# Attention in two matmul forms: products of 64 columns per query block, or split products of 256 and 384 columns per key block, with more weights split ahead of the joins

## The chip, the cores and the metric

One core of a Trainium2 chip runs the whole kernel. The metric is device microseconds of that core for one execution, as the median of several runs. The engines are named as in the profile: PE multiplies matrices, DVE, ACT and POOL work on vectors, SP starts transfers.

## The reference

Two layers of an encoder on an input of 512 rows x 1024, all in fp32. Each layer adds three blocks to x, each with a norm before it and one behind:

```
x = x + 0.5 * rms_norm(swiglu(rms_norm(x, nw[0]), ...), nw[1])
m = even_mixer(...) if l % 2 == 0 else odd_mixer(...)
x = x + rms_norm(m, nw[3])
x = x + 0.5 * rms_norm(swiglu(rms_norm(x, nw[4]), ...), nw[5])
```

swiglu has 2816 inner columns. The even mixer joins a pooling of 256 columns with attention: 12 query heads of 64 columns, 4 heads of keys and values, and each block of 128 queries sees the blocks before, at and behind it, with a sink term in the denominator:

```
m = jnp.maximum(jnp.max(s, axis=-1, keepdims=True), sk)
p = jnp.exp(s - m)
denom = jnp.sum(p, axis=-1, keepdims=True) + jnp.exp(sk - m)
o = jnp.einsum('bnhgqk,bnkhd->bnqhgd', (p / denom).astype(v.dtype), vw)
```

The odd mixer joins a gated convolution with a state-space scan in two directions, whose output y becomes rms_norm(y * silu(z)).

## The kernel before, in words

The stages run in the order f00 (FFN), even mixer, f01, f10, odd mixer, f11. x lives in SBUF as four row blocks of 128. An fp32 matrix product is done as three products of rounded halves (mm3: high x high, high x low, low x high), each through mm. split makes the halves of an activation: ACT casts the high half (xh), DVE subtracts it for the low half (xl). Weights come through one queue of blocks, class Stream: a DMA brings a raw block, pump has ACT cast it (whi, L118) and DVE subtract (wlo, L119). The function keep marks blocks that an earlier FFN splits instead; pump writes those halves to DRAM and reads them back at their turn. Before, such blocks are those of the two mixers alone (KEEP 6 and 24).

Nothing is issued as the code stands: each part is a generator that yields either a time to wait (in ns of PE cost, counted as matmuls are issued: CHAIN, PWAIT, AVWAIT, UWAIT), or an event, or Need(n), n free ones of the eight PSUM banks. A planner runs the generators against that count, and so writes the order of instructions of every engine. Each engine then runs its own order, and waits on semaphores of the others.

Attention, in even(): heads goes over six pairs of query heads c and four query blocks n. unit(c, n) issues the scores of both heads (ev_s), the maxima (mx, L679), the bias (nm, L680), the exponentials with their sums (ev_p, L684), the sink terms (ex, L689), sum and reciprocal (rs, L691 and L692), the transposes of the probabilities by 128x128 blocks (ev_pT), their copies to SBUF (ev_pTs, L702 on ACT, L704 on DVE), the products with the values in plain fp32 (ev_av, 64 columns each, the probabilities as the stationary side), and the scaling by the reciprocal (ev_o, L715). Up to DEPTH = 3 units are under way at once. pair_end transposes the four outputs of a pair (ev_oT) and splits them into two row blocks of the mixer's output (ev_mh, ev_ml). Projections (ev_q, ev_u) and the output projection (evo_y) run between the units.

At the end of a stage down calls finish for each row block: squares (L462), the weighted copy (L463), the norm's factor (rstd, L428 on DVE, L430 on POOL), the addition to x (L471). norm_t follows with the next stage's norm (L438, L440), waits CHAIN[kind], and issues the transposes (evon_tp after the even mixer) and their split (L402). f_g and f_u are the FFN's matmuls behind them. wrow loads the norm's weight rows, and halves those of an FFN on POOL.

In odd(), the z projection (od_z) is made of four blocks of 256 columns for four row blocks, each evicted in 256 columns (L1190, L1174).

Of the kernel before, what the change touches and what calls it, by code (L numbers as in the profile page):

```python
# [7 lines left out]
F32 = mybir.dt.float32  # L8
# [22 lines left out]
DEPTH = 3  # L31
CHAIN = (12500, 8000, 13000)
# [10 lines left out]
ESPLIT = (3, 3)  # L43
# [7 lines left out]
ZBATCH = (4, 8)  # L51
# [3 lines left out]
KEEP = (6, 24)  # L55
DWB, LNG, LNB, CVB, CVW = 0, 4, 8, 12, 28
# [167 lines left out]
def odd_blocks(d):  # L224
# [16 lines left out]
    for b in range(4):  # L241
        out.append(dict(key=("z", b), src=w[:, :, 1024 + 256 * b:1280 + 256 * b], shape=(KC, 256),
                        parts=[(slice(0, 4), full(256)), (slice(4, 8), full(256))]))
# [22 lines left out]
class Gen:  # L266
# [151 lines left out]
    def wrow(self, src, name, half):  # L418
# [6 lines left out]
    def rstd(self, ss, n, name):  # L425
# [29 lines left out]
    def finish(self, t, src, banks, wpost, wnext, scratch, name, eng, kind):  # L455
# [11 lines left out]
        r = self.rstd(s1, D, f"{name}_p{t}")  # L467
# [142 lines left out]
    def even(self):  # L610
# [3 lines left out]
        with ExitStack() as es:  # L614
# [23 lines left out]
            v = [T(f"v{t}", [P, 256]) for t in range(NT)]  # L638
# [13 lines left out]
            def unit(c, n, av):  # L652
# [9 lines left out]
                ps, pss = [], []  # L662
                scs = []
# [18 lines left out]
                for e in range(2):  # L682
                    p = T("p", [P, 384], name=f"p{c}_{n}{e}", bufs=2 * DEPTH)
# [9 lines left out]
                self.free(*scs)  # L693
                yield PWAIT[c > 0]
                yield Need(2)
                for e in range(2):
                    pT = self.psum(f"ev_pT{c}_{n}{e}")
                    for b in range(nk // P):
                        self.tp(pT, pT[:, b * P:(b + 1) * P], ps[e][:, b * P:(b + 1) * P])
                    pTs = T("pTs", [P, 384], name=f"pTs{c}_{n}{e}", bufs=4)  # L700
                    if e == 0:
                        nc.scalar.copy(out=pTs[:, :nk], in_=pT[:, :nk])  # L702
                    else:
                        nc.vector.tensor_copy(out=pTs[:, :nk], in_=pT[:, :nk])  # L704
                    self.free(pT)
                    pss.append(pTs)
# [6 lines left out]
                o = T("o", [P, P], name=f"o{c}_{n}", bufs=2 * NT)  # L713
                for e in range(2):
                    nc.vector.tensor_scalar(out=o[:, 64 * e:64 * e + 64], in0=av[:, n * P + 64 * e:n * P + 64 * e + 64],  # L715
                                            scalar1=rs[:, e:e + 1], scalar2=0.0, op0=ALU.mult, op1=ALU.add)
                self.os[c, n] = o

            def heads():

                us = []
                for c in range(6):
                    yield qready[c]
                    yield Need(1)
                    av = self.psum(f"ev_av{c}")
# [7 lines left out]
            def pair_end(c, av, us):  # L733
                for u in us:
                    yield u
                self.free(av)
                yield 600
                yield Need(1)
                oT = self.psum(f"ev_oT{c}")
                for n in range(NT):  # L740
                    self.tp(oT, oT[:, n * P:(n + 1) * P], self.os.pop((c, n)))
                self.split(mix[2 + c][0], mix[2 + c][1], oT)
                self.free(oT)
                yield 1200
                mready[2 + c].done = True
# [8 lines left out]
            def pool(c, p):  # L754
                u = T("u", [P, 16 + S + 16], name=f"u{c}", bufs=2)
                a = T("sa", [P, 16 + S + 16], name=f"sa{c}", bufs=2)
# [37 lines left out]
            self.os, fa = {}, {}  # L794
# [10 lines left out]
            for t in range(NT):  # L805
# [3 lines left out]
                nc.scalar.copy(out=v[t], in_=pv[:, 0:256])  # L809
# [56 lines left out]
    def odd(self):  # L866
# [6 lines left out]
        with ExitStack() as es:  # L873
# [293 lines left out]
            zw = {}  # L1167

            def zblock(b, t):
# [3 lines left out]
                sz = self.scr.tile([P, 256], F32, tag="sg", name=f"od_sz{b}{t}")  # L1173
# [226 lines left out]
```

## Time and profile before

| what | us |
|---|---|
| median of 3 runs (lowest, highest) | 2007.65 (2005.86, 2009.3) |
| the profiled execution | 2007.16 |
| its span, from the first to the last instruction | 2005.4 |
| PE busy | 1980.2 |
| DVE busy | 971.3 |
| ACT busy | 761.8 |
| POOL busy | 64.5 |

The mean granted clock of PE is 0.996 of full speed. The page gives busy time and the chain of work that ended last, the windows give both for a stretch, and the lines give groups of instructions with their mean time and what ended the idle time before them. Matmuls overlap in the pipeline, so the mean time of a record is longer than the step from one to the next; steps are read from the chain.

### The profile page before, as it was taken

The page shows a single profiled execution, that of the slowest core. Times are in us where ns is not written, and L with a number is a line of the kernel's source. Part 1 is how long each engine was busy: PE and PEld are TensorE (multiplying, and loading weights), DVE is VectorE, ACT ScalarE, POOL GpSimd, SP SyncE. Part 2 cuts the span into 40 slices and gives each one's busy share as a digit, 9 for nine tenths or more (in the row PEclk, how much of TensorE's full clock was granted, in tenths as well). Part 3 has the DMA queues.
Part 4 walks back from the last instruction along what each step waited for, and adds up shares of the span by engine and source line. Part 5 has one row for each costly group of instructions (what it writes and reads, how often), then busy time and mean ns, then how long its engine had stood idle before and what let it go on. Part 6 is the DMA issues. An engine that isn't in the chain of part 4 may idle for free.

```text
span 2005.4 us, 25194 instructions
## 1 busy us (share of the span) xinstructions
PE 1980.2 (99%) x10257; PEld 1682.4 (84%) x10257; DVE 971.3 (48%) x1436; ACT 761.8 (38%) x1246; POOL 64.5 (3%) x94
## 2 busy tenths in 40 slices
PE   8999999999999999999999999999999999999998
PEld 7888888988888888888988888898889888888886
DVE  5434444556355334436444344569997254223334
ACT  5333333266334244234334333346655233232231
POOL 1000000011110000001000000000000010000000
PEclk9999999999999999999999999999999999999999
DMA  7757674351317577742567574254333623323321
GB/s 236 226 163 231 212 250 146 140 190 43 106 64 236 171 251 246 237 168 95 172 246 243 209 252 164 95 213 147 106 126 106 220 74 105 105 84 106 93 76 42
DMA packets 192315, 320.58 MB, mean 160 GB/s; under 512 B 22640, under 2 KB 142536, under 8 KB 192200
## 3 DMA queue, kind: packets, MB, share of 16 engines
q1 hardware_dynamic: 192200, 318.99, 47.2%
q8 instruction: 80, 1.31, 0.3%
q14 instruction: 35, 0.29, 0.0%
HBM read 249.49 MB, written 69.47 MB: 159 GB/s over the span
## 4 chain that ended last, share of the span: by engine, by line
PE 93%; DVE 3%; ACT 2%; POOL 1%; issue 1%; DMA 0%; SPq 0%; POOLq 0%; DVEq 0%; ACTq 0%
PE f_g L338 24%; PE f_u L338 24%; PE f_y L338 24%; PE od_bc L338 2%; PE od_ab L338 2%; PE od_xs L338 2%; PE odo_y L338 2%; PE od_z L338 2%; PE evo_y L338 1%; PE ev_av L338 1%; PE ev_s L338 1%; PE ev_q L338 1%; PE od_yd L338 1%; PE ev_pT L353 1%; PE od_sc L338 1%
## 5 line engine op out<-in xcount | busy, mean ns | idle before, releaser
L119 DVE TENSOR_TENSOR wlo<-raw,whi 128x1024 fp32r<-128x1024 f32 x329 | 400.5, 1221 | 617.0 <-ACT whi L118 525.0
L118 ACT CAST whi<-raw 128x1024 fp32r<-128x1024 f32 x329 | 344.4, 1051 | 865.6 <-PE f_g L338 263.7
L338 PE MATMUL f_g<-xl,whi 128*128 128x512 f32 (+1 forms) x832 | 297.6, 358 | 1.7 <-DVE xl L402 1.4
L338 PE MATMUL f_g<-xh,whi 128*128 128x512 f32 (+1 forms) x832 | 297.8, 358 | 0.6 <-ACT xh L401 0.6
L338 PE MATMUL f_g<-xh,wlo 128*128 128x512 f32 (+1 forms) x832 | 297.2, 357 | 0.0
L338 PE MATMUL f_u<-xh,whi 128*128 128x512 f32 (+1 forms) x768 | 286.4, 373 | 0.2 <-DVE xl L402 0.2
L338 PE MATMUL f_u<-xl,whi 128*128 128x512 f32 (+1 forms) x768 | 285.9, 372 | 0.0
L338 PE MATMUL f_u<-xh,wlo 128*128 128x512 f32 (+1 forms) x768 | 285.9, 372 | 0.0
L338 PE MATMUL f_y<-whi,f_hh 128*128 128x512 f32 x704 | 274.4, 390 | 0.0
L338 PE MATMUL f_y<-whi,f_hl 128*128 128x512 f32 x704 | 273.9, 389 | 0.0
L338 PE MATMUL f_y<-wlo,f_hh 128*128 128x512 f32 x704 | 273.9, 389 | 0.0
L338 PEld LDWEIGHTS f_g<-xl,whi 128*128 128x128 f32 x832 | 157.9, 190 | 24.9 <-DVE xl L402 1.9
L338 PEld LDWEIGHTS f_g<-xh,whi 128*128 128x128 f32 x832 | 157.8, 190 | 23.8 <-ACT xh L401 1.3
L338 PEld LDWEIGHTS f_g<-xh,wlo 128*128 128x128 f32 x832 | 158.0, 190 | 22.4
L338 PEld LDWEIGHTS f_u<-xh,whi 128*128 128x128 f32 x768 | 145.4, 189 | 25.3 <-DVE xl L402 0.4
L338 PEld LDWEIGHTS f_u<-xl,whi 128*128 128x128 f32 x768 | 145.5, 189 | 24.8
L338 PEld LDWEIGHTS f_u<-xh,wlo 128*128 128x128 f32 x768 | 145.4, 189 | 24.9
L338 PEld LDWEIGHTS f_y<-whi,f_hl 128*128 128x128 f32 x704 | 132.2, 188 | 27.4
L338 PEld LDWEIGHTS f_y<-wlo,f_hh 128*128 128x128 f32 x704 | 132.2, 188 | 27.3
L338 PEld LDWEIGHTS f_y<-whi,f_hh 128*128 128x128 f32 x704 | 132.2, 188 | 27.2
L566 DVE TENSOR_TENSOR f_hf<-f_sg,f_u 128x512 f32<-128x512 f32 x88 | 60.4, 686 | 185.9 <-PE f_u L338 185.3
L922 DVE SCALAR_TENSOR_TENSOR od_ca<-od_glu,od_dww,od_ca 128x499 f32<-128x499 f32 (+14 forms) x120 | 87.5, 736 | 0.6
(378 smaller groups left out, 2475.0 us busy)
## 6 DMA issues: line engine op xcount, KB each, us to landing
raw<-ffn_w_up SPq DMA_DIRECT2D x44, 1024.0 KB, 5.4
raw<-ffn_w_down SPq DMA_DIRECT2D x44, 1024.0 KB, 5.0
raw<-ffn_w_gate SPq DMA_DIRECT2D x43, 1024.0 KB, 5.4
raw<-od_w_in SPq DMA_DIRECT2D x16, 512.0 KB, 5.4
raw<-od_w_in SPq DMA_DIRECT2D x8, 1024.0 KB, 6.1
raw<-od_w_out SPq DMA_DIRECT2D x6, 1024.0 KB, 6.0
raw<-ev_w_in SPq DMA_DIRECT2D x3, 1024.0 KB, 5.4
raw<-ev_w_in SPq DMA_DIRECT2D x12, 256.0 KB, 4.0
```

The costliest lines, as they stand in the source:

```text
L118: g.later(nc.scalar.copy(out=hv, in_=src), 0)
L119: g.later(nc.vector.tensor_tensor(out=lv, in0=src, in1=hv.bitcast(F32), op=ALU.subtract), 1)
L338: self.seq(bank, self.nc.tensor.matmul(reg, a, b, start=start, stop=stop, skip_group_check=True))
L353: self.seq(bank, self.nc.tensor.transpose(out=reg, in_=a, identity=self.ident[0:n, 0:n]))
L566: nc.vector.tensor_tensor(out=h, in0=sg, in1=pu, op=ALU.mult)
L922: V.scalar_tensor_tensor(out=o[:, lo:hi], in0=t[:, lo + sh:hi + sh], scalar=dww[:, k * 4 + g:k * 4 + g + 1], in1=o[:, lo:hi], op0=ALU.mult ...
```

## The change

1. unit ends with the scaling of the probabilities themselves (L693 after the change). A new part, keyblock(c, kb), transposes the probabilities of all query blocks that see key block kb, splits them into halves, and multiplies with the values, split as well, as the stationary side: three products per head, 256 columns wide at the ends and 384 in the middle, summed over key blocks in one PSUM bank per head. The transposes of the outputs go; pair_end splits the 64 used rows of either bank. The limit DEPTH goes; a unit of pair c waits until key block n of the pair before has been transposed.
2. The first three weight blocks of the FFN behind either mixer are kept too (EARLY = 6 halves), CHAIN has two values per stage by row block, and ESPLIT is (3, 2).
3. The halving of weight rows on POOL moves into the constants of rstd.
4. The z projection has two halves of 512 columns.

The diff, cut to its core (left out: the pooling's buffers, one of each instead of two, the blocks and evictions of z, and unchanged lines):

```diff
-DEPTH = 3
-CHAIN = (12500, 8000, 13000)
+CHAIN = ((12500, 12500), (6500, 11500), (7000, 13000))
-ESPLIT = (3, 3)
+ESPLIT = (3, 2)
-ZBATCH = (4, 8)
+ZBATCH = (2, 4)
+EARLY = 6
...
-        if half:
-            self.nc.gpsimd.tensor_scalar(out=t, in0=t, scalar1=0.5, scalar2=0.0, op0=ALU.mult, op1=ALU.add)
...
-        nc.vector.tensor_scalar(out=m, in0=ss, scalar1=1.0 / n, scalar2=EPS, op0=ALU.mult, op1=ALU.add)
+        nc.vector.tensor_scalar(out=m, in0=ss, scalar1=div * div / n, scalar2=div * div * EPS, op0=ALU.mult, op1=ALU.add)
...
-            yield from self.norm_t(t, self.x[t], wnext, scratch, self.xh, self.xl, name + "n", CHAIN[kind], True)
+            yield from self.norm_t(t, self.x[t], wnext, scratch, self.xh, self.xl, name + "n", CHAIN[kind][t > 1], True)
...
-            v = [T(f"v{t}", [P, 256]) for t in range(NT)]
+            v = [tuple(T(f"v{x}{t}", [P, 256], F32R) for x in "hl") for t in range(NT)]
...
                 nc.vector.reciprocal(out=rs, in_=rs)
                 self.free(*scs)
+                for e in range(2):
+                    nc.vector.tensor_scalar(out=ps[e][:, :nk], in0=ps[e][:, :nk], scalar1=rs[:, e:e + 1], scalar2=0.0, op0=ALU.mult, op1=ALU.add)
+                self.probs[c, n] = ps
+                turned[c, n] = Event()
+
+            def keyblock(c, kb, prev):
+
+                n0, n1 = max(kb - 1, 0), min(kb + 1, NT - 1)
+                w = (n1 - n0 + 1) * P
                 yield PWAIT[c > 0]
-                yield Need(2)
+                if prev:
+                    yield prev
+                if kb == 0:
+                    yield Need(2)
+                    avs[c] = [self.psum(f"ev_av{c}_{e}") for e in range(2)]
+                pT = []
                 for e in range(2):
-                    pT = self.psum(f"ev_pT{c}_{n}{e}")
-                    for b in range(nk // P):
-                        self.tp(pT, pT[:, b * P:(b + 1) * P], ps[e][:, b * P:(b + 1) * P])
...
+                    yield Need(1)
+                    px = self.psum(f"ev_pT{c}_{kb}{e}")
+                    for j, n in enumerate(range(n0, n1 + 1)):
+                        b = kb - max(n - 1, 0)
+                        self.tp(px, px[:, j * P:(j + 1) * P], self.probs[c, n][e][:, b * P:(b + 1) * P])
+                    hl = [T(f"pT{x}", [P, 384], F32R, name=f"pT{x}{c}_{kb}{e}", bufs=3) for x in "hl"]
+                    self.split(hl[0][:, :w], hl[1][:, :w], px[:, :w])
+                    self.free(px)
+                    pT.append(hl)
+                if kb:
+                    turned[c, kb - 1].done = True
...
                 yield AVWAIT
+                cols = slice(P * (c // 3), P * (c // 3) + P)
                 for e in range(2):
-                    kv = PAIRS[c][e] // 3
-                    for b in range(nk // P):
-                        self.mm(av, av[:, n * P + 64 * e:n * P + 64 * e + 64], pss[e][:, b * P:(b + 1) * P],
-                                v[b0 + b][:, kv * 64:(kv + 1) * 64], b == 0, b == nk // P - 1)
...
+                    bank = avs[c][e]
+                    self.mm3(bank, bank[:, n0 * P:(n1 + 1) * P], (v[kb][0][:, cols], v[kb][1][:, cols]),
+                             (pT[e][0][:, :w], pT[e][1][:, :w]), kb == 0, kb == NT - 1)
 
             def heads():
...
                     for n in range(NT):
-                        if len(us) >= DEPTH:
-                            yield us[-DEPTH]
-                        us.append(self.spawn(unit(c, n, av)))
+                        if c:
+                            yield turned[c - 1, n]
+                        yield self.spawn(unit(c, n))
+                        for kb in ([n - 1] if n else []) + ([n] if n == NT - 1 else []):
+                            kbs.append(self.spawn(keyblock(c, kb, kbs[-1])))
                         yield UWAIT
-                    fa[c] = self.spawn(pair_end(c, av, us[-4:]))
...
+                    fa[c] = self.spawn(pair_end(c, kbs[-1]))
+
+            def pair_end(c, last):
+                yield last
+                for e in range(2):
+                    r = slice(64 * e, 64 * e + 64)
+                    self.split(mix[2 + c][0][r], mix[2 + c][1][r], avs[c][e][r])
+                self.free(*avs.pop(c))
+                yield 1800
                 mready[2 + c].done = True
...
-                nc.scalar.copy(out=v[t], in_=pv[:, 0:256])
+                self.split(*v[t], pv[:, 0:256])
...
+            def ztile(h, w, t, free=False):
+
                 yield Need(1)
-                pz = self.psum(f"od_z{b}{t}")
-                yield from self.tok(pz, zw[b], t)
...
+                pz = self.psum(f"od_z{h}{t}")
+                for k in range(KC):
+                    wh, wl = w[k // 2]
+                    self.mm3(pz, pz, (self.xh[:, k, t * P:(t + 1) * P], self.xl[:, k, t * P:(t + 1) * P]),
+                             (wh[:, k % 2, :], wl[:, k % 2, :]), k == 0, k == KC - 1)
...
-                lists[seq[m]] = keep(lists[seq[m]], [lists[s] for s in seq[a:b] if s[0] == "f"])
+                nxt, n = lists[seq[m + 1]], EARLY // 2
+                split = keep(lists[seq[m]] + nxt[:n], [lists[s] for s in seq[a:b] if s[0] == "f"])
+                lists[seq[m]], nxt[:n] = split[:-n], split[-n:]
```

The order on DVE in attention, in the fourth and fifth pair (names end in pair, query block and head). Before:

```order
L679 TENSOR_REDUCE mx4_10_4411<-ev_s4_10_4401 128x1
L679 TENSOR_REDUCE mx4_11_4416<-ev_s4_11_4402 128x1
L680 TENSOR_SCALAR nm4_1_4400<-mx4_10_4411,ev_nsink_3106 128x1
L680 TENSOR_SCALAR nm4_1_4400<-mx4_11_4416,ev_nsink_3106 128x1
L691 TENSOR_TENSOR rs4_0_4372<-rs4_0_4372,ex4_0_4394 128x2
```

With the change:

```order
L677 TENSOR_REDUCE mx3_00_4310<-ev_s3_00_4301 128x1
L678 TENSOR_SCALAR nm3_0_4300<-mx3_00_4310,ev_nsink_3159 128x1
L677 TENSOR_REDUCE mx3_01_4314<-ev_s3_01_4302 128x1
L678 TENSOR_SCALAR nm3_0_4300<-mx3_01_4314,ev_nsink_3159 128x1
L689 TENSOR_TENSOR rs3_0_4299<-rs3_0_4299,ex3_0_4321 128x2
L690 RECIPROCAL rs3_0_4299<-rs3_0_4299 128x2
L693 TENSOR_SCALAR ev_p3_00_4317<-ev_p3_00_4317,rs3_0_4299 128x256
L693 TENSOR_SCALAR ev_p3_01_4319<-ev_p3_01_4319,rs3_0_4299 128x256
L403 TENSOR_TENSOR ev_pTl2_20_4351<-ev_pT2_20_4346,ev_pTh2_20_4350 128x384
L403 TENSOR_TENSOR ev_pTl2_21_4359<-ev_pT2_21_4354,ev_pTh2_21_4358 128x384
L677 TENSOR_REDUCE mx3_10_4374<-ev_s3_10_4364 128x1
```

Before, the maxima of the next query block stand ahead of the sum of the block before it; with the change the sum (rs) of a block stands right behind its own bias (nm), and the next block's maxima behind the subtractions of a key block.

The order on PE for the products with the values, in the fifth pair. Before, in products of 64 columns:

```order
L338 MATMUL ev_av4_4280<-ev_v0_3122,ev_pTs4_00_4474 128x64
L338 MATMUL ev_av4_4280<-ev_v1_3123,ev_pTs4_00_4474 128x64
L338 MATMUL ev_av4_4280<-ev_v0_3122,ev_pTs4_01_4479 128x64
L338 MATMUL ev_av4_4280<-ev_v1_3123,ev_pTs4_01_4479 128x64
L338 MATMUL ev_s4_30_4536<-ev_kh1_3120,ev_mh6_3093 128x256
```

With the change, in split products of 256 columns, between matmuls of the output projection (evo_y) and transposes of the next key block:

```order
L339 MATMUL ev_av4_0_4711<-ev_pTl4_00_4717,ev_vh0_3175 128x256
L339 MATMUL ev_av4_0_4711<-ev_pTh4_00_4716,ev_vl0_3176 128x256
L339 MATMUL ev_av4_1_4712<-ev_pTh4_01_4723,ev_vh0_3175 128x256
L339 MATMUL ev_av4_1_4712<-ev_pTl4_01_4724,ev_vh0_3175 128x256
L339 MATMUL ev_av4_1_4712<-ev_pTh4_01_4723,ev_vl0_3176 128x256
L354 MATMUL ev_pT4_10_4733<-ident_94,ev_p4_00_4551 128x128
L354 MATMUL ev_pT4_10_4733<-ident_94,ev_p4_10_4610 128x128
L354 MATMUL ev_pT4_10_4733<-ident_94,ev_p4_20_4661 128x128
```

A transposed tile now takes one block from each of three query blocks, so it stands behind all three of their softmaxes.

## Rows read from the trace of the kernel before

**Rows 1.** The page: busy time of each engine, and the chain by engine.
```profile
PE 1980.2 (99%) x10257; PEld 1682.4 (84%) x10257; DVE 971.3 (48%) x1436; ACT 761.8 (38%) x1246; POOL 64.5 (3%) x94
...
PE 93%; DVE 3%; ACT 2%; POOL 1%; issue 1%; DMA 0%; SPq 0%; POOLq 0%; DVEq 0%; ACTq 0%
```

**Rows 2.** Waits of PE: us in total, times, longest.
```profile
PE evon_tp L353 <- DVE ev_s L440: 2.6, 1, 2.6
PE f_g L338 <- DVE xl L402: 1.4, 2, 0.8
```

**Rows 3.** Windows, first FFN and attention: length, busy time (instructions), PEclk, DMA share, GB/s.
```profile
core 0: us, PE busy (x) PEld busy (x) DVE busy (x) ACT busy (x) POOL busy (x), PEclk, DMA share, GB/s
...
30.00:378.00 348.00, 348.00 (x1626) 291.88 (x1626) 147.54 (x163) 122.29 (x157) 3.80 (x6) 1.00 0.59 191
...
400.00:516.00 116.00, 115.00 (x884) 98.83 (x883) 69.60 (x232) 71.71 (x209) 19.84 (x19) 1.00 0.31 114
```

**Rows 4.** The chain of waits: start, length, what ran, number of instructions.
```profile
476.87 1.48 PE ev_av L338 x12
...
513.32 1.83 PE ev_s L338 x16
...
517.93 1.09 PE ev_pT L353 x10
...
529.47 19.10 PE evo_y L338 x84
...
1492.96 4.31 PE od_z L338 x36
```

**Rows 5.** Lines of PE, 400 to 530 us: busy, mean ns, idle before.
```profile
L338 PE MATMUL ev_av<-ev_v,ev_pTs 128*128 128x64 f32 x240 | 30.5, 273 | 0.1
```

**Rows 6.** Lines of DVE, 400 to 520 us.
```profile
L679 DVE TENSOR_REDUCE mx<-ev_s 128x1 f32<-128x256 f32 (+1 forms) x48 | 21.6, 481 | 1.7 <-PE ev_s L338 1.6
L704 DVE COPY ev_pTs<-ev_pT 128x256 f32<-128x256 f32 (+1 forms) x24 | 11.4, 482 | 4.3 <-PE ev_av L338 2.7 <-PE ev_pT L353 1.6
L715 DVE TENSOR_SCALAR ev_o<-ev_av,rs 128x64 f32<-128x64 f32 x44 | 10.9, 277 | 13.4 <-PE ev_av L338 13.4
L680 DVE TENSOR_SCALAR nm<-mx,ev_nsink 128x1 f32<-128x1 f32 x48 | 8.4, 204 | 0.0
L691 DVE TENSOR_TENSOR rs<-rs,ex 128x2 f32<-128x2 f32 x24 | 4.4, 182 | 6.9 <-ACT ex L689 6.6
...
L692 DVE RECIPROCAL rs<-rs 128x2 f32<-128x2 f32 x24 | 3.8, 158 | 0.3
L402 DVE TENSOR_TENSOR ev_ml<-ev_oT,ev_mh 128x512 fp32r<-128x512 f32 x5 | 3.4, 685 | 0.0
```

**Rows 7.** Two scalar products of DVE in the odd mixer: min/median/max ns.
```profile
L917 DVE TENSOR_SCALAR od_ca<-od_glu,od_dww,od_cols x4: 535/541/547, 1329.7 to 1467.6; 128x512 f32<-128x512 f32 x4
...
L1241 DVE TENSOR_SCALAR od_rstdb<-ones,od_var_s x4: 279/286/286, 1551.0 to 1554.3; 128x128 f32<-128x128 f32 x4
```

**Rows 8.** Timeline of one unit's exponentials: start, length, instruction.
```profile
504.83 0.47 ACT L684 ACTIVATE ev_p<-ev_s,nm 128x256 f32<-128x256 f32 x1 [1.20 <-DVE nm L680]
...
505.92 0.29 ACT L689 ACTIVATE ex<-ev_sink,nm 128x1 f32<-128x1 f32 x1
```

**Rows 9.** The chain of waits at the even join.
```profile
565.74 1.22 DVE wlo L119
566.96 1.81 DVE xl L402 x3
568.81 7.26 PE f_g L338 x46
```

**Rows 10.** Windows of 2 us at the even join.
```profile
568.00:570.00 2.00, 1.19 (x10) 1.20 (x11) 1.41 (x4) 2.00 (x6) 0.45 (x1) 0.99 0.00 0
570.00:572.00 2.00, 2.00 (x12) 2.00 (x11) 1.86 (x1) 2.00 (x4) 1.13 (x2) 0.50 0.00 0
572.00:574.00 2.00, 2.00 (x14) 2.00 (x14) 2.00 (x4) 0.36 (x1) 0.00 (x0) 0.66 0.00 0
```

More of the change, by code (lines that the diff above doesn't have):

```diff
@@ L241, in odd_blocks @@
     for b in range(4):
-        out.append(dict(key=("z", b), src=w[:, :, 1024 + 256 * b:1280 + 256 * b], shape=(KC, 256),
-                        parts=[(slice(0, 4), full(256)), (slice(4, 8), full(256))]))
+        c = 1024 + 512 * (b // 2)
+        out.append(dict(key=("z", b), src=w[:, 4 * (b % 2):4 * (b % 2) + 4, c:c + 512], shape=(4, 512),
+                        parts=[(slice(0, 2), full(512)), (slice(2, 4), full(512))]))
     for b in range(6):
@@ L650, in rope, with unit @@
                 self.split(hl[0], hl[1], t1)
-            def unit(c, n, av):
+            def unit(c, n):
                 qh, ql = qT[c]
@@ L1165, in odd, with zparts @@
                 fs.append(self.spawn(start(g, Bc, Cc, xs, preps[g])))
-            zw = {}
-            def zblock(b, t):
+            def zparts(h):
+                return [st.get(("z", 2 * h + i // 2, i % 2)) for i in range(4)]
+            def ztile(h, w, t, free=False):
                 yield Need(1)
-                pz = self.psum(f"od_z{b}{t}")
-                yield from self.tok(pz, zw[b], t)
-                sz = self.scr.tile([P, 256], F32, tag="sg", name=f"od_sz{b}{t}")
-                A.activation(out=sz, in_=pz[:, 0:256], func=AF.Silu)
-                self.free(pz)
-                yv = y[t][:, 256 * b:256 * b + 256]
-                V.tensor_tensor(out=yv, in0=yv, in1=sz, op=ALU.mult)
@@ L1180, in odd @@
-            held = []
-            for b in range(2):
-                zw[b] = [st.get(("z", b, j)) for j in range(2)]
-                for t in range(NT):
-                    if t % 2 == 0:
-                        q = T(f"glu{len(held)}", [P, S], name=f"zr{b}{t}")
-                        held.append((b, t, q))
-                    yield Need(1)
-                    pz = self.psum(f"od_z{b}{t}")
-                    yield from self.tok(pz, zw[b], t)
-                    V.tensor_copy(out=q[:, 256 * (t % 2):256 * (t % 2) + 256], in_=pz[:, 0:256])
-                    self.free(pz)
-                    if b * NT + t + 1 in ZBATCH:
-                        for _, _, q in held:
-                            A.activation(out=q, in_=q, func=AF.Silu)
-                        for zb, t0, q in held:
-                            for i in range(2):
-                                yv = y[t0 + i][:, 256 * zb:256 * zb + 256]
-                                V.tensor_tensor(out=yv, in0=yv, in1=q[:, 256 * i:256 * i + 256], op=ALU.mult)
-                        held = []
-                st.put(2)
+                pz = self.psum(f"od_z{h}{t}")
@@ new lines, in ztile @@
+                for k in range(KC):
+                    wh, wl = w[k // 2]
+                    self.mm3(pz, pz, (self.xh[:, k, t * P:(t + 1) * P], self.xl[:, k, t * P:(t + 1) * P]),
+                             (wh[:, k % 2, :], wl[:, k % 2, :]), k == 0, k == KC - 1)
+                    if k % 2:
+                        if free:
+                            st.put()
+                        yield
+                return pz
+            held, w = [], zparts(0)
+            for t in range(NT):
+                q = T(f"glu{t}", [P, S], name=f"zr{t}")
+                held.append((t, q))
+                pz = yield from ztile(0, w, t, t == NT - 1)
+                V.tensor_copy(out=q, in_=pz)
+                self.free(pz)
+                if t + 1 in ZBATCH:
+                    for _, q in held:
+                        A.activation(out=q, in_=q, func=AF.Silu)
+                    for tt, q in held:
+                        V.tensor_tensor(out=yall[:, tt, 0:512], in0=yall[:, tt, 0:512], in1=q, op=ALU.mult)
+                    held = []
@@ L1251, in odd @@
             fln = self.spawn(layer_norm())
-            for b in range(2, 4):
-                zw[b] = [st.get(("z", b, j)) for j in range(2)]
+            w1 = zparts(1)
             hold, fy = {}, []
@@ L1265, in odd @@
             for t in range(NT):
-                for b in range(2, 4):
-                    yield from zblock(b, t)
+                pz = yield from ztile(1, w1, t, t == NT - 1)
+                sz = self.scr.tile([P, S], F32, tag="sg", name=f"od_sz{t}")
+                A.activation(out=sz, in_=pz, func=AF.Silu)
+                self.free(pz)
+                V.tensor_tensor(out=yall[:, t, 512:1024], in0=yall[:, t, 512:1024], in1=sz, op=ALU.mult)
                 fy.append(self.spawn(ynorm(t)))
-            st.put(4)
             def lhs(c):
@@ L1314, in row @@
                 l, j = s[1], {"f": (0, 4), "m": (2,)}[s[0]][s[2] if s[0] == "f" else 0] + (which == "post")
-                return d["norm_w"][l, j], f"w{which}_{'_'.join(map(str, s))}", which == "post" and s[0] == "f"
+                return d["norm_w"][l, j], f"w{which}_{'_'.join(map(str, s))}"
             e0 = es.enter_context(ExitStack())
```

49 lines of the change are left out of this document (12 added, 37 removed).

## The prediction

> **What bounds the kernel now.** I read the page first: PE is busy for 1980.2 us of the 2005.4 us span, and PE makes up 93% of the chain that ended last [rows 1]. So the time is PE's own work plus a few places where it waits, and an edit counts only if it takes work off PE, takes away a wait of PE, or makes one. The view of waits lists them: at the even join PE waits 2.6 us for a normalised tile to transpose and 1.4 us for the low half of one [rows 2]; what else it lists is the start of the program, which the change does not touch, and small change. The windows by stage then tell how much room the other engines have. In the attention stretch, 400 to 516 us, PE is busy 115.0 of 116 us while DVE and ACT are busy for 69.60 and 71.71; in the first FFN both are busy under half the time and the DMA engines 0.59 of it [rows 3]. The reader is to see that attention has no PE idle time today, though its softmax runs through DVE and ACT: work of other units and of projections fills every gap.
>
> **The base.** All sums go against the profiled execution, 2007.16 us (span 2005.4); the median of the runs shown, 2007.65, lies 0.5 above it. A difference of 0.2%, 4 us, is about what a measurement of this kernel can tell from no change.
>
> **Probabilities times values, PE's side.** Before, 120 products of 64 columns in plain fp32 leave 240 records; the chain has 12 of them in 1.48 us, 123 ns each [rows 4], so 240 cost 29.6 us (their busy time, with the modelled ends, is 30.5 [rows 5]). The change issues 144 split products instead: per pair of heads four key blocks x two heads x three products, half of 256 columns and half of 384. The 256-column price is 120 ns (36 od_z in 4.31 us), the 512-column price 227 ns (84 evo_y in 19.10) [rows 4]; 384 lies halfway, 174 ns. 72 x 0.120 + 72 x 0.174 = 21.1 us: a gain of 8.5. The 24 transposes of the outputs go as well, at the 109 ns of a transpose (10 in 1.09 us [rows 4]): 2.6. All of it lies on PE, so **-11.1**.
>
> **Its other side: DVE and ACT.** Per unit (two heads, one query block) DVE did two maxima (481 ns, mean of both widths), two bias steps (204), one sum (182), one reciprocal (158), one copy of the transposed probabilities (482) and two scalings of the output (277) [rows 6]: 2.75 us. Now it does maxima, bias, sum and reciprocal as before (1.71), two scalings of the probabilities, and two subtractions for the low halves. The subtractions read the same PSUM tiles as the old copy: 482 each. The scalings have no row of their own; the nearest are the scalar products of 128x128 and 128x512 elements, 286 and 541 ns [rows 7]; those are the bounds, and the line between them gives 370 and 455 for 256 and 384 columns, mean 412, which I take. Together 3.50 us a unit, 14.0 a pair, and two subtractions of 685 [rows 6] where a pair ends make 15.4.
>
> The Trainium skill, page "VectorE: DVE Perf Modes" (Mode 2×_2P and the cycle table behind it), has fp32 scalar products from SBUF to SBUF at two elements a cycle; its cycle table gives, as an estimate, 0.23 us for the mean of these widths. By it the 412 ns would fall by 0.18, and the time below by 4.4 us (24 scalings in the last three pairs). The rows speak against it [rows 7]: the narrow one, of 128 columns, already costs 286 ns, and their time grows by 0.67 ns a column; so the rows' price stands.
>
> PE's own work in a pair is: scores 4 x 0.915 (two units in 1.83 us [rows 4]), 20 transposes, 2.2, and the new products, 3.5: 9.4 us. What fills the rest is, by the order of instructions, 36, 36 and 48 matmuls of 512 columns beside pairs 0 to 2, but only 12, 13 and 25 beside pairs 3 to 5. So PE has 17.6, 17.6, 20.3 and then **12.1, 12.4 and 15.1 us** of work in them. The lower bound of the new wait is that DVE's 15.4 us are all that counts: 3.3 + 3.0 + 0.3 = 6.6 us. The upper bound is that each unit goes round in series: scores 0.92, first maximum and bias 0.69, both exponentials with their sink terms 1.38 (from 504.83 to 506.21 us, of 256 columns [rows 8]) and 0.11 more in the mean of the widths, sum and reciprocal 0.34, two scalings 0.82, two subtractions 0.96: 5.2 us, 20.8 a pair. Against PE's work that is 8.7 + 8.4 + 5.7 = 22.8 in pairs 3 to 5, and 3.2 + 3.2 + 0.5 more, 29.7, if pairs 0 to 2 go round like that too.
>
> I take it nearer the upper end, for a reason that the order shows: on DVE the sum of a unit stands right behind its bias steps, with nothing between, so DVE itself stands still for the 1.4 us of the exponentials, where before it had another unit's maxima or copies in that place. The output sums of the first two row blocks hold four of the eight PSUM banks and the products of the pair two, so the next scores need the banks that the transposes leave. Pairs 4 and 5 interleave two units once each, which saves a wait of 1.4 us each: 22.8 - 2.8 = **+20**. Pairs 0 to 2 I cost at nothing: 36 and more filling matmuls cover them; if not, it is the 6.9 above.
>
> **The z projection.** 384 products of 256 columns (46.1 us at 120 ns) become 192 of 512 (43.5 at 227): **-2.6**. Its evictions are half as many and twice as wide, and PE has no long wait for them now.
>
> **The even join.** The chain: PE ends the output projection of the first row block at 548.57 (529.47 + 19.10 [rows 4]), then norm steps run in series on ACT, DVE and POOL, a weight's low half (1.22) goes ahead of the last low half of the activations, and f_g starts at 568.8: 20.2 us [rows 9]. PE has 72 matmuls and 16 transposes for that time, 18.1 us. After the change the weights there come ready from DRAM, so the 1.22 goes: 19.0. But the first row block ends with the attention and the second 12 matmuls behind it, so PE has 60 matmuls and 16 transposes, 15.4 us: a wait of 3.6. The third block's transposes, which wait 2.6 today [rows 2], stand behind 87 matmuls (19.7 us) and should wait no more. Today's idle time is followed by half clock: 1.19 of 2 us busy at 568, then a granted clock of 0.50 and 0.66 [rows 10], worth 1.0 + 0.7 = 1.7 us, and once more after the second wait. So 2.6 + 1.4 + 3.4 = 7.4 becomes 3.6 + 1.7 = 5.3: **-2.1**, between +1.5 (its waits stay and one more dip comes) and -5.
>
> **At nothing.** The twelve more kept parts (six a join) go to DRAM and back: their casts and subtractions move from the mixers into FFNs where ACT and DVE are busy 0.35 and 0.42 of the time, and DMA has 0.41 left [rows 3]; if that cover failed, a transfer would be late at the join. POOL's halving of weight rows and the split of v lie beside PE work.
>
> **Clock in attention.** The new waits are short, but there are many. I put in one dip and a little, **+2**, between 0 and 11 (rival below).
>
> **Sum.** -11.1 + 20 - 2.6 - 2.1 + 2 = +6.2: 2007.2 + 6.2 = **2013.4 us**.
>
> **Rivals.**
> - *Covered* (the other side): the waits for the exponentials are filled, and only DVE's busy time counts, 6.6 instead of 20, no dip: 2007.2 - 11.1 + 6.6 - 2.6 - 2.1 = **1998.0**. For it speaks that today's attention loses nothing to a softmax of the same length; against it the order, where the units no longer overlap, and the few filling matmuls late. It decides below a stall of some 12 us. Chance 0.25.
> - *Half-way*: pairs 3 to 5 lose 10 to 16 us and the whole is within 4 us of now, near **2006**. Chance 0.17.
> - *Half clock*: the waits hold the granted clock down through pairs 3 to 5. Today's dip comes behind a stretch in which PE was busy for 1.19 of 2 us [rows 10], and a unit that goes round in 5.2 us with 3 to 4 of PE work has such idle. Then scores double in the ring: 12 x 0.92 = 11 us more, **2024**. Chance 0.13. The Trainium skill, page "TensorE: Matmul & The Clock Gate" (A second HAM failure mode: psum-queue depth-cycling), has such short idle between matmul groups switching the clock to and fro; by that rule this rival holds, and the rows show it so far at the join alone.
> - *The change does not do what it says*: kept weights land late at a join and PE waits for DMA instead of DVE; at 3 to 5 us on top of the forecast, **2017**. Chance 0.05.
>
> **How the numbers follow.** Forecast 0.40 (its own range 2008 to 2019). Faster by over 0.2%: the first rival, 0.25, and 0.01 of half-way with the join's better end: 0.26. Within 0.2%: the rest of half-way, 0.16, and 0.03 of the forecast's lower edge: 0.19. Slower: the rest of the forecast, 0.37, half clock 0.13 and late weights 0.05: 0.55. The range reaches from the first rival to the third, 1996 to 2024.
>
> **What would show it.** In the profile after: ev_av with 144 records at 120 and 174 ns; od_z with 192; DVE busy in attention some 22 us more; waits of PE for DVE and ACT at ev_s, ev_pT and ev_av that add to about 20 us in the last three pairs, and none at the third block's transposes in the join. Wrong if PE stays at 99% between the first scores and the last output product: then the first rival holds, and the step "the sum right behind the bias" has cover that I did not see.

## The result, and the profile after

The change makes the kernel slower: 2026.59 us in the median of 6 runs (2020.94 to 2031.25) against 2007.82 (2005.86 to 2009.78); the ratio is 1.0092, 95% interval 1.0071 to 1.0113. The forecast was 2013.4 us, in a range of 1996 to 2024: the direction was right, the size was too small, and the median lies above the range. The runs with the change spread over 10 us where those before spread over 4. Three had a mean granted clock of 0.996 and took 2020.9 to 2024.2 us, three had 0.991 and took 2028.9 to 2031.3. The profiled execution, 2024.24 us, is of the first kind.

The page of the change, busy time of each engine (answers to [rows 1]):

```profile
PE 1987.9 (98%) x9945; PEld 1667.6 (82%) x9945; DVE 995.7 (49%) x1458; ACT 775.3 (38%) x1272; POOL 59.2 (3%) x90
```

DVE has 24 us more to do in all, and 25.6 in the six pairs of attention (88.3 against 62.7 in the windows below); the forecast said some 22 there. Where the 17.1 us of the span go is read by cutting both traces at the same events: from the start to the last product of the first FFN +1.9 (the first f_g ran at half clock in this run, and in some of the experiments whatever their edit, so this is the run's and not the change's); from the first score to the first matmul of the FFN behind the mixer **+19.6**; from there to that FFN's first down product -3.4; all the rest -1.0.

Windows of the change: the first three pairs of attention, the last three, the stretch with the low clock, and the wait at the join (PE busy 1.46 of 4 us); columns as in [rows 3]:

```profile
428.40:491.50 63.10, 58.49 (x335) 43.21 (x334) 45.16 (x134) 39.83 (x119) 17.05 (x21) 1.00 0.29 108
491.50:559.30 67.80, 61.19 (x321) 43.18 (x321) 43.15 (x132) 33.84 (x109) 0.00 (x0) 0.95 0.03 8
522.00:530.00 8.00, 7.81 (x30) 5.36 (x30) 5.80 (x18) 3.53 (x11) 0.00 (x0) 0.58 0.00 0
588.00:592.00 4.00, 1.46 (x9) 1.14 (x8) 3.16 (x7) 2.05 (x5) 0.55 (x1) 0.94 1.01 377
```

The same six pairs in the kernel before, cut after the third:

```profile
426.50:474.90 48.40, 47.45 (x340) 38.19 (x339) 32.34 (x112) 33.79 (x105) 3.82 (x3) 1.00 0.24 86
474.90:524.70 49.80, 49.75 (x379) 41.95 (x378) 30.38 (x118) 25.92 (x91) 12.58 (x16) 1.00 0.15 54
```

130.9 us instead of 98.2. In the change 174 filling matmuls of 512 columns run in that time, before some 120; 54 x 0.227 = 12.3 us of the difference are work that only moved, and 20.4 are lost, with what the products save already taken off. PE is idle for 11 us of it and at a clock of 0.58 for 8 us (worth 3.4). The rest doesn't show as idle time. The likely reason is that records of matmuls overlap, so that a short wait can lie inside a busy record; no run shows this by itself. The waits of PE in attention are many and small:

```profile
PE ev_pT L354 <- ACT ev_p L682: 1.7, 3, 1.1
PE ev_py L339 <- ACT ev_p L682: 1.2, 1, 1.2
PE ev_av L339 <- ACT ev_p L682: 1.1, 1, 1.1
PE ev_s L339 <- ACT ev_p L682: 1.1, 2, 0.7
PE ev_pT L354 <- DVE ev_p L693: 1.1, 1, 1.1
PE ev_av L339 <- ACT ev_pTh L402: 1.1, 5, 0.3
PE ev_av L339 <- DVE ev_pTl L403: 0.8, 3, 0.4
```

At the join behind it one wait is left:

```profile
PE f_g L339 <- DVE xl L403: 2.3, 1, 2.3
```

On DVE the lines of the same stretch answer to [rows 6]:

```profile
L677 DVE TENSOR_REDUCE mx<-ev_s 128x1 f32<-128x256 f32 (+1 forms) x48 | 22.1, 484 | 8.5 <-PE ev_s L339 8.3
L403 DVE TENSOR_TENSOR ev_pTl<-ev_pT,ev_pTh 128x256 fp32r<-128x256 f32 (+1 forms) x48 | 21.9, 483 | 5.2 <-ACT ev_pTh L402 4.9
L693 DVE TENSOR_SCALAR ev_p<-ev_p,rs 128x256 f32<-128x256 f32 (+1 forms) x48 | 18.1, 419 | 0.5
...
L689 DVE TENSOR_TENSOR rs<-rs,ex 128x2 f32<-128x2 f32 x24 | 4.7, 194 | 21.0 <-ACT ex L687 20.8
```

The scalings cost 419 ns (estimated 412) and the subtractions 483 (482). DVE stands still for 20.8 us ahead of the sums, where before it was 6.6: that is the order "the sum right behind the bias". That by itself doesn't say that PE waits because of it.

### The profile page after: what moved, and what is told of

The parts are those of the page before. It is cut to its first block, busy times and chain, and to the rows that moved or that the text cites. A ratio compares the mean times of both kernels' runs of the same rounds, so it can differ in the third digit from the quotient of the medians.

```text
span 2022.5 us, 24707 instructions
## 1 busy us (share of the span) xinstructions
PE 1987.9 (98%) x9945; PEld 1667.6 (82%) x9945; DVE 995.7 (49%) x1458; ACT 775.3 (38%) x1272; POOL 59.2 (3%) x90
## 4 chain that ended last, share of the span: by engine, by line
PE 91%; DVE 4%; ACT 2%; issue 1%; POOL 1%; DMA 0%; SPq 0%; POOLq 0%; DVEq 0%; ACTq 0%
PE f_g L339 24%; PE f_u L339 24%; PE f_y L339 24%; PE od_bc L339 2%; PE od_ab L339 2%; PE od_xs L339 2%; PE od_z L339 2%; PE odo_y L339 2%; PE evo_y L339 1%; PE ev_s L339 1%; PE od_yd L339 1%; PE ev_av L339 1%; PE ev_q L339 1%; PE od_sc L339 1%; PE od_yo L339 1%
## 5 line engine op out<-in xcount | busy, mean ns | idle before, releaser
L119 DVE TENSOR_TENSOR wlo<-raw,whi 128x1024 fp32r<-128x1024 f32 (+1 forms) x329 | 399.6, 1222 | 561.1 <-ACT whi L118 436.2
L118 ACT CAST whi<-raw 128x1024 fp32r<-128x1024 f32 (+1 forms) x329 | 344.3, 1051 | 813.6 <-PE f_g L339 249.2
```

What stands on the lines that cost most here:

```text
L118: g.later(nc.scalar.copy(out=hv, in_=src), 0)
L119: g.later(nc.vector.tensor_tensor(out=lv, in0=src, in1=hv.bitcast(F32), op=ALU.subtract), 1)
```

## The experiments

**Two halves.** join_only is the change with attention and ESPLIT as before:

```diff
-ESPLIT = (3, 2)
+ESPLIT = (3, 3)
...
-            def keyblock(c, kb, prev):
+            def unit(c, n, av):
```

> The change with attention as it was before (plain products of 64 columns, three units under way, ESPLIT 3,3); all else of the change stays. If the serial softmax of the new attention is what costs, this is faster than before by what the trace of the change shows behind attention: 3.4 us at the even join and 1.1 in the z projection, so 2001 to 2006 us. If the kept weights and the new join cost something (late transfers), it is 2008 to 2015. With the old ESPLIT the old order of the first two row blocks comes back, so the join may gain less than 3.4.

Measured 1999.29 us (1997.54 to 2001.51), ratio 0.9959 (0.9946 to 0.9971): the change without the new attention is a gain of 8.2 us, and this is the fastest version of the study. attn_only is the other half, the kernel before with the new attention and ESPLIT 3,2:

> The kernel before with the new attention alone (and ESPLIT 3,2, since six banks for the output projection leave too few for the new products). If the new attention is the whole cost: 2007.8 plus 19.6 us of the stretch and 0 to 8 us of clock, 2024 to 2036. If half of the cost came from the join's new weights: about 2018. Its attention stretch should be as long as in the change, 160 us from the first scores to the last output product.

Measured 2035.31 us, ratio 1.0137 (1.0123 to 1.0152). 27.8 - 8.2 = 19.6, against the 18.8 of both together: the halves add up, and all of the loss comes with the new attention and its ESPLIT (ESPLIT 3,2 with the old attention was not run). Its six pairs are 131.0 us long, as in the change.

**The scalings.** no_scale leaves out the division of the probabilities:

```diff
-                for e in range(2):
-                    nc.vector.tensor_scalar(out=ps[e][:, :nk], in0=ps[e][:, :nk], scalar1=rs[:, e:e + 1], scalar2=0.0, op0=ALU.mult, op1=ALU.add)
```

> The change without the 48 scalings of the probabilities on DVE, so its output lacks the division by the denominator. Serial theory: each unit's round loses two scalings (364 or 474 ns each in the trace of the change, 18.1 us in all), and the wait for the reciprocal too, since the transposes no longer need it (0.4 us and the exponentials of the sink): 10 to 18 us come back, 2009 to 2017. DVE as a whole the bound: 18 us less busy time gives the same, so the two are told apart by DVE's idle time: in the serial case DVE stays idle for over a third of attention. If the clock or PE's own steps are the cost: 2022 or more.

Measured 2015.66 us, ratio 1.0039 (1.0026 to 1.0053): 11 us came back, as the serial theory wanted. The windows, cut at the same events, show where:

```profile
428.70:486.80 58.10, 54.89 (x327) 42.18 (x327) 35.51 (x110) 40.11 (x119) 12.18 (x15) 1.00 0.31 117
486.80:553.90 67.10, 59.88 (x329) 43.93 (x329) 35.34 (x108) 33.85 (x109) 4.45 (x7) 0.95 0.03 9
```

DVE has 17.5 us less to do. The last three pairs take 67.1 us instead of 67.8, with 8 filling matmuls more (1.8 us), the first three 58.1 instead of 63.1, with 8 fewer. For the same work that is 2.5 us and 3.2 us. So the scalings are a small part of the round in the last three pairs (2.5 of the 9.8 us that 12 units at 0.82 would give back), and they do count in the first three, which the forecast had at nothing. The rest of the 11 us is not attention's: in the profiled executions 1.4 come at the join and some 2 in the odd mixer, and the runs of no_scale lie within 0.6 us of each other, those of the change within 10.

**The banks.** esplit31 lets the early output projection hold two PSUM banks instead of four:

```diff
-ESPLIT = (3, 2)
+ESPLIT = (3, 1)
```

> The change with the early part of the output projection for one row block instead of two: it holds two PSUM banks instead of four while attention runs, and offers half the filling matmuls (36 instead of 72). If the banks are what forces the units into series: units overlap again in pairs 3 to 5 and 5 to 12 us come back, 2015 to 2022. If the lack of filling matmuls is what shows: it gets worse by up to 36 x 0.227 = 8 us, 2027 to 2035.

Measured 2013.88 us (2013.52 to 2014.74), ratio 1.0030 (1.0019 to 1.0041): 12.7 back, and the spread between runs is gone. The first and the last three pairs:

```profile
429.00:490.00 61.00, 55.82 (x324) 41.40 (x323) 43.99 (x129) 38.50 (x115) 16.86 (x21) 1.00 0.30 111
490.00:545.50 55.50, 47.81 (x296) 36.42 (x296) 41.82 (x137) 33.79 (x114) 0.14 (x1) 0.97 0.03 11
```

The last three are 12.3 us shorter, with 24 filling matmuls fewer (5.4 us). Those run behind attention instead, so the fair measure is the whole stretch from the first scores to the first matmul of the FFN behind the mixer, which holds the same work in all (789 or 790 records of matmuls). Here it is of the change, of esplit31, and of one_bank32 below, which keeps ESPLIT 3,2:

```profile
428.40:588.40 160.00, 148.55 (x790) 110.12 (x789) 100.59 (x286) 82.11 (x249) 19.25 (x25) 0.98 0.22 81
429.00:582.70 153.70, 140.59 (x790) 108.35 (x789) 99.48 (x288) 81.07 (x249) 19.76 (x26) 0.99 0.24 86
428.60:582.30 153.70, 144.94 (x789) 110.63 (x788) 96.10 (x280) 77.52 (x243) 19.25 (x25) 0.98 0.23 85
```

With two more banks the units go round faster, by 6.3 us. Another 3.6 us of the 12.7 come at the join, since ESPLIT 3,1 also changes the order there: from the first matmul of that FFN to its first down product it is 94.8 us in the change, 91.2 in esplit31. esplit31_pool adds the scalings on POOL (gpsimd instead of vector in that line):

> ESPLIT 3,1, two banks, and the 48 scalings on POOL, which does nothing else in pairs 3 to 5. DVE loses 18 us of work. If DVE's busy time bounds attention once the banks are freed: 5 to 10 us less than esplit31, 2004 to 2009. If the round of scores, exponentials, transposes and splits through the banks still bounds it: 2011 to 2015; POOL being slower, the next key block's transposes may come late: up to 2022.

Measured 2013.64 us, no difference from esplit31. But the two halves of attention differ, at the same number of filling matmuls:

```profile
428.20:485.30 57.10, 53.76 (x323) 41.44 (x322) 34.27 (x107) 39.27 (x118) 23.13 (x36) 1.00 0.32 119
485.30:545.60 60.30, 50.21 (x296) 38.65 (x296) 35.85 (x111) 33.87 (x111) 18.85 (x34) 0.92 0.03 10
```

The first three pairs gain 3.9 us, as in no_scale. The last three lose 4.8: a scaling takes 479 or 607 ns on POOL against 364 or 474 on DVE, PE waits 4.1 us for POOL's, and the clock is lower (0.92 against 0.97). So this run doesn't show that the round there is free of the scalings. one_bank31 and one_bank32 put both heads' products into one bank:

```diff
-                    avs[c] = [self.psum(f"ev_av{c}_{e}") for e in range(2)]
+                    avs[c] = self.psum(f"ev_av{c}")
...
-                cols = slice(P * (c // 3), P * (c // 3) + P)
...
+                    h = 192 * (c // 3) + 64 * e
+                    cols = slice(h, h + P)
```

> The change with ESPLIT 3,1 and the products of both heads of a pair in one PSUM bank instead of two (the values beside 64 columns of zeros, so that each head adds nothing to the other's rows; two instead of three buffers for the split probabilities make room). PE's work is the same; one or two more banks are free in attention, and a pair ends in one split of 128 rows instead of two of 64, 0.7 us less on DVE and 0.6 on ACT a pair. If banks still bind at ESPLIT 3,1: 4 to 8 us less than with two banks, 2006 to 2010. If they do not any more: 2011 to 2015, or above where the two buffers bind.

> The same with ESPLIT 3,2 as in the change: the filling matmuls of the change (72, not 36) and one or two banks more. If banks and not filling matmuls are the cause: 2014 to 2019, since 3.5 us of the join's gain stay away with this ESPLIT. If the order within a unit is the cause whatever the banks: 2024 to 2029 as the change.

Measured 2010.69 us (ratio 1.0014, 1.0005 to 1.0024) and 2017.02 us (1.0045, 1.0028 to 1.0062). At ESPLIT 3,2 that is 9.6 us less, at 3,1 only 3.2. In the stretch of the same work it is 6.3 and 0.4, but one_bank31 ran its last three pairs at a lower clock than esplit31 (0.88 against 0.97):

```profile
485.00:543.30 58.30, 53.40 (x299) 40.96 (x299) 40.96 (x134) 32.37 (x113) 1.54 (x3) 0.88 0.03 10
```

So banks are a cause at ESPLIT 3,2, where two edits that free them gave 6.3 us each. (This edit also ends a pair in one split instead of two.) Whether they still bind at 3,1, the clock hides. one_bank_late goes to the end of it (ESPLIT 0,1, no early output projection):

> One bank a pair, and no early output projection at all: attention has seven banks for itself in pairs 3 to 5, and no filling matmul of the output projection beside it (36 of 0.227 us more behind it than with ESPLIT 3,1). If banks are still what binds: the three pairs, 58 us with ESPLIT 3,1, come down to the 41 us that DVE is busy in them, and less the 8.2 us moved behind, 2001 to 2006. If a unit's own round and the late filling matmuls bind: 2010 to 2018.

Measured 2018.49 us (2017.15 to 2023.31). Its last three pairs are no shorter than the 58.3 us of one_bank31, with 21 filling matmuls fewer, and PE works at a clock of 0.82, so it can't answer that either:

```profile
483.40:541.40 58.00, 51.54 (x280) 38.96 (x280) 40.75 (x140) 32.98 (x113) 2.99 (x5) 0.82 0.03 10
```

**What the round is made of.** pT_const lets the transposes read a constant table, av_const lets the products read constant halves:

```diff
-                        self.tp(px, px[:, j * P:(j + 1) * P], self.probs[c, n][e][:, b * P:(b + 1) * P])
+                        self.tp(px, px[:, j * P:(j + 1) * P], cos[:, b * P:(b + 1) * P])
...
-                             (pT[e][0][:, :w], pT[e][1][:, :w]), kb == 0, kb == NT - 1)
+                             (kT[0][0][:, :w], kT[0][1][:, :w]), kb == 0, kb == NT - 1)
```

> The change with the transposes reading a constant table instead of the probabilities, so that they depend on no exponential and no scaling; all else is issued as before, and attention's output is not the reference's. If a unit's round is set by the transposes waiting for the softmax (the theory of the forecast: exponentials, sum, scalings, then transposes): pairs 3 to 5, 67.8 us in the change, come down to 48 to 56, and the time to 2004 to 2014. If the round goes through the PSUM banks (scores wait for the banks of the transposes, transposes for the banks of the scores) and the order on DVE: 60 us or more there, 2016 to 2028.

> The change with the products reading constant halves instead of the split transposes, so that no product waits for ACT's cast or DVE's subtraction; the output is not the reference's. If those waits, and products at the head of PE's queue that hold up the scores behind them, set the round: pairs 3 to 5 lose 6 us or more, 2013 to 2020. If they lie beside the round: within 3 us of the change, 2022 to 2030.

pT_const: 2026.66 us, ratio 1.0097 (1.0076 to 1.0117), the change to a tenth of a microsecond, and its last three pairs too:

```profile
491.60:559.40 67.80, 61.18 (x322) 43.26 (x322) 43.13 (x133) 33.85 (x109) 0.00 (x0) 0.95 0.01 3
```

No transpose needs a probability there, and nothing gets faster. Of the waits of its transposes the row for DVE's scaling (1.1 us) is gone, and the row for the exponential stands as it was:

```profile
PE ev_pT L354 <- ACT ev_p L682: 1.7, 3, 1.1
```

So that row is no wait for data. What it can be is a wait for a bank: the exponential is the last reader of the scores' bank, which the transposes are to be written into. av_const: 2017.11 us, ratio 1.0047 (1.0031 to 1.0064):

```profile
491.40:551.40 60.00, 55.91 (x315) 41.71 (x314) 41.90 (x129) 32.45 (x107) 0.00 (x0) 0.94 0.00 1
```

7.8 us less in the last three pairs, at the same clock (2 filling matmuls fewer). So the products' wait for cast and subtraction is in the round. As the trace shows it, the round is: scores, maxima and bias, exponentials (which free the banks), transposes into those banks, cast, products that wait for the cast at the head of PE's queue, subtraction (which frees the banks again, and stands on DVE behind the scalings of the next unit), next scores behind the products. In the change's timeline one round reads, on ACT, DVE and PE (PEld, the loading of the stationary side, in one row alone):

```profile
515.15 0.47 ACT L682 ACTIVATE ev_p<-ev_s,nm 128x256 f32<-128x256 f32 x1 [0.20 <-DVE nm L678]
...
515.77 0.55 PE L354 MATMUL ev_pT<-ident,ev_p 128*128 128x128 f32 x3 [0.40 <-ACT ev_p L682]
515.80 1.09 ACT L402 CAST ev_pTh<-ev_pT 128x384 fp32r<-128x384 f32 x2
...
516.33 0.62 DVE L693 TENSOR_SCALAR ev_p<-ev_p,rs 128x256 f32<-128x256 f32 x2
516.87 1.02 DVE L403 TENSOR_TENSOR ev_pTl<-ev_pT,ev_pTh 128x384 fp32r<-128x384 f32 x2
516.95 0.44 PE L339 MATMUL ev_av<-ev_pTh,ev_vh 128*128 128x384 f32 x1 [0.18 <-ACT ev_pTh L402]
517.47 0.18 PEld L339 LDWEIGHTS ev_s<-ev_kh,ev_mh 64*128 64x128 f32 x1 [0.34 <-DVE ev_pTl L403]
517.47 0.44 PE L339 MATMUL ev_s<-ev_kh,ev_mh 64*128 64x384 f32 x1
```

The scores of 517.47 wait for the first subtraction, begun at 516.87 (the row of PEld names it); they use none of its data, so this too is a wait for its bank. ob_pw70 moves the transposes further behind by the planner's waits (PWAIT 7000, AVWAIT 3000, on one_bank31):

> One bank a pair, ESPLIT 3,1, with the planner's waits ahead of transposes and products raised (PWAIT 7000 instead of 2500 for all pairs but the first, AVWAIT 3000 instead of 2250), so that a unit's transposes stand further behind its exponentials in PE's order. On DVE the sum then stands one unit later in half of the units. If PE's waits come from transposes that the planner sets too early: 3 to 6 us less, 2005 to 2008. If the dependence itself binds (a key block needs three units): 2009 to 2015.

Measured 2010.01 us, no difference: its last three pairs are 49.5 us long instead of 58.3, at a clock of 1.00 instead of 0.88, but the first three 63.6 instead of 58.3, with the same number of filling matmuls; 2.6 us of that is one wait for POOL's pooling (ev_py).

**The joining change.** Three kernels with attention and ESPLIT as before, and all with z in halves: z_only has no kept weights and the old constants, no_early only the new constants, old_chain only the kept weights (the first edit is in z_only and old_chain, the second in z_only and no_early):

```diff
-CHAIN = ((12500, 12500), (6500, 11500), (7000, 13000))
+CHAIN = ((12500, 12500), (8000, 8000), (13000, 13000))
...
-                split = keep(lists[seq[m]] + nxt[:n], [lists[s] for s in seq[a:b] if s[0] == "f"])
-                lists[seq[m]], nxt[:n] = split[:-n], split[-n:]
+                lists[seq[m]] = keep(lists[seq[m]], [lists[s] for s in seq[a:b] if s[0] == "f"])
```

> The kernel before with the z projection in halves of 512 columns and POOL's halving removed, and nothing else: no kept weights, old constants, old attention. The trace of the change says 1 us for z; the prediction said 2.6. So 2005 to 2007, and the kept weights with the new constants are then worth the other 6 of the 8.2 us of join_only. If z was worth them: 1999 to 2002.

> Old attention, z in halves, the new constants of the norms' waits, but no weights of the FFNs kept ahead (EARLY 0). If the constants alone make the join's gain: 1999 to 2001. If the kept weights make it: 2005 to 2009, since without them the weights' casts and subtractions stand in the way again at the join.

> Old attention, z in halves, the kept weights, but the old constants (8000 and 13000 for all row blocks). If the kept weights alone make the gain: 1999 to 2002, less perhaps the 2.6 us wait of the third block's transposes. If only both together: 2004 to 2008.

Measured 2007.12 us (ratio 0.9998, 0.9989 to 1.0008), 2000.13 (0.9967, 0.9955 to 0.9980) and 1999.95 (0.9964, 0.9951 to 0.9977). The z projection is worth nothing that can be measured; the constants alone and the kept weights alone are each worth about 7 us, and both together 8. From the first matmul of the FFN behind the mixer to its first down product, the profiled executions take 98.2 us in z_only, 93.5 in no_early, 93.2 in old_chain and 91.3 in join_only; some 2 us of the 7 lie outside the join. The waits of PE at the join, of z_only, no_early and old_chain in this order:

```profile
PE evon_tp L355 <- DVE ev_s L440: 2.6, 1, 2.6
...
PE f_g L340 <- DVE xl L404: 1.4, 2, 0.8
```

```profile
PE f_g L340 <- DVE xl L404: 2.2, 3, 1.1
...
PE evon_tp L355 <- DVE ev_s L440: 1.2, 1, 1.2
```

```profile
PE evon_tp L355 <- DVE ev_s L440: 1.7, 1, 1.7
PE f_g L340 <- DVE xl L404: 0.9, 2, 0.8
```

and the windows of the join, first z_only, then no_early:

```profile
560.00:580.00 20.00, 18.73 (x115) 16.80 (x114) 15.90 (x23) 10.77 (x21) 3.04 (x4) 0.91 0.36 113
580.00:600.00 20.00, 17.36 (x134) 17.18 (x133) 4.78 (x7) 4.79 (x8) 0.55 (x1) 0.91 0.14 47
```

```profile
560.00:580.00 20.00, 18.67 (x134) 17.23 (x132) 15.32 (x23) 11.37 (x22) 3.95 (x5) 1.00 0.41 139
580.00:600.00 20.00, 18.83 (x158) 18.59 (x157) 7.79 (x9) 8.01 (x11) 0.54 (x1) 1.00 0.13 34
```

z_only has both of the dips to half clock that the kernel before has; no_early has none, though it waits nearly as long. 2 x 20 x 0.09 = 3.6 us of the gain are clock.

## Why the prediction was right in direction and wrong in size

- **The step that failed: "Pairs 0 to 2 I cost at nothing: 36 and more filling matmuls cover them".** The filling matmuls are there (36, 36 and 50), and the three pairs took 63.1 us where the forecast had 55.5 of PE's work. The two numbers don't hold quite the same work, since the last products of pair 2 fall into the next window (54 and 90 records of ev_av, 50 and 70 of ev_pT). Priced at the steps of [rows 4] by the records in each window, the change is 11.0 us over its matmuls in the first three pairs and 24.1 in the last three; the kernel before is 3.3 and 0.5 over. So pairs 0 to 2 lost 7.7 us, near the 6.9 that the text kept as an end of the range, and pairs 3 to 5 lost 23.6, where the forecast had 20 and 2 for the clock. For the six pairs the forecast had -11.1 + 20 + 2 = +10.9; the trace shows +20.4, and most of the difference is pairs 0 to 2. Some 3 to 4 us of their loss go with DVE's scalings (no_scale, esplit31_pool); what makes up the rest is open.
- **The round in pairs 3 to 5** came out near in size, 23.6 us against 20 and 2, but partly by luck, since it was wrong in parts: the scalings were in it at 9.8 us (0.82 a unit), and without them 2.5 came back; the transposes and ACT's cast were not in it, and the rows of pT_const (the wait for the bank) and av_const (7.8 us) show that they are. That "the next scores need the banks that the transposes leave" holds, by the scores of 517.47 and by the 6.3 us that spared banks gave. That DVE stands still for the exponentials is true (20.8 us); no run moved the sum by itself, so whether PE waits for that is open.
- **The prices.** Scalings and subtractions came out as taken, and DVE's extra work a little higher (25.6 for 22). The products can't be read alone, since waits lie between them. z was taken at -2.6; z_only shows 0.3, with an interval that includes nothing. A step of 120 ns for 256 columns against 227 for 512 was too thin a basis for a gain.
- **The even join** was forecast at -2.1 with one dip left; the trace of the change shows -3.4, one wait of 2.3 us ahead of f_g and one dip. Its waits at the third block's transposes are gone, as said. The forecast had the reason, the 12 matmuls that ESPLIT 3,2 leaves between the first two row blocks. What it didn't see is how much more there was to gain: with another ESPLIT that wait and that dip are gone too, in join_only (91.3 us against 94.8 and, before, 98.2) and in esplit31 with the new attention (91.2).
- **The clock.** The rival "half clock", at 2024 us, held in part: a dip of about 8 us in pair 4 in the profiled run, and, by the mean clocks, more in half of the runs, which are some 8 us slower. I had put +2 for it. The Trainium skill, page "TensorE: Matmul & The Clock Gate" (A second HAM failure mode: psum-queue depth-cycling), by whose rule that rival went, says that short idle between groups of matmuls that cycle through PSUM banks switches the clock to and fro. This trace agrees with it once, in pair 4 (a clock of 0.58 from 522 to 530 us). That banks are the reason, these runs don't show: no_scale holds the same banks as the change and its runs lie within 0.6 us of each other, while one_bank_late has the most banks free and the lowest clock (0.82). None of the three runs at 0.991 was profiled, so where their low clock falls is open.
- **The rival "covered"**, 1998 us, fell: PE is not at 99% in attention (busy 119.7 of 130.9 us). The faster time that it named is the one of join_only, by another way.

What stays open: with more banks free, the six pairs still take 113 to 117 us in esplit31, one_bank31 and ob_pw70, some 25 to 29 us more than their matmuls at the steps of [rows 4], where the kernel before takes 4 more. That a key block needs three units at once, and with that the planner's order, is the likely reason; it was only argued.

## What to carry to other kernels

Fewer and wider products are worth what PE saves only while other units fill the waits: count the PSUM banks that each unit in flight holds, and what holds the others meanwhile, before pricing the products. A wait that the profile puts down to an instruction can be for its bank and not for its data; replacing the data by a constant tells which. Runs that move work out of a window are compared over a stretch that holds the same instructions. A rewrite that comes with a good change is timed apart from it: here one half gained 8 us and the other lost 28.

## What was not expected

Two unrelated edits, the constants and the kept weights, give nearly the same 7 us each and 8 together. Either removes the two stretches of half clock at the join (PEclk 0.91 and 0.91 in z_only, 1.00 and 1.00 in no_early), and that is the larger part of what they have in common. The length of a single wait doesn't tell whether a dip follows: in z_only one dip came behind the wait of 2.6 us and one behind a wait of 0.8 at f_g, while no_early's waits of 1.1 and 1.2 and old_chain's of 1.7 were followed by none. And the same program ran with two mean clocks, 0.996 and 0.991, in six runs, some 8 us apart.
